# A decoder layer on one core: the cached keys and values of two head groups multiplied on GpSimd, summed on VectorE with a transposition in blocks, and TensorE adding four partial sums

## The chip, the cores and the metric

The kernel runs on 1 core of one Trainium2 chip, as one launch. The metric is the device time of that core in microseconds (us). Before the change it is 1753.67 us, the median of 3 runs (1753.51 to 1753.68).

## The reference, cut to what matters

One layer of a decoder is computed for 256 prompt tokens and for 32 sample tokens (8 sequences, "batches", of 4 new tokens each) that share all weights: one input projection (2048 to 14848 features), a gated short convolution (mixer A), attention with three head groups of 4 heads of 128 features (mixer B), two gated branch projections, an output projection, a layer norm, and a feed-forward part with 5632 inner features and a second norm. All arrays are float32.

The change concerns the sample tokens' attention to their caches. For each batch `n`, new token `t` and head `h`, a group with window 128 and dilation `dil` reads every `dil`-th earlier row:

```python
idx = l + jnp.arange(t)[:, None] - dil * j[None, :]      # j = 0 .. 128
kg = k_all[:, idx]
vg = v_all[:, idx]
sc = jnp.einsum('nthd,ntjhd->nhtj', q, kg) * ATT_SCALE - slopes * (dil * j)
...
o = jnp.einsum('nhtj,ntjhd->nthd', p / den, vg)
```

In the first group (dilation 1) the 4 new tokens of a batch share their keys and values. In groups two and three (dilations 4 and 16) each of the 4 tokens has 128 cached rows of its own, which no other token of the batch reads. So in these two groups every element of the cache that is read is multiplied with one number only: the query's feature for the keys, the softmax weight for the values. All three groups are merged by one softmax per head. The caches themselves are also outputs (moved on by four rows), so each cached element is copied once from the inputs to the outputs.

## The kernel before, in words

**Products.** Tokens lie along the free dimension (288 columns: 256 prompt, 32 sample), features on the 128 partitions. Every projection is a row of *products* (`product`, which calls `mms`): one block of 128 output features, usually 2048 inputs, so 16 blocks of 128x128. Each block takes three matmuls of 288 columns (L223 to L225), since a float32 weight is split into two float32r parts, `whi` and `wlo`, and the inputs likewise into `xh` and `xl`; so a product of 2048 inputs has 48 matmuls.

**Weights.** `prepare` loads one weight block of 1 MB by a DMA that SyncE issues (L186; tile `wst`, three buffers), and `half_block` splits it in two halves: ScalarE writes `whi` (L229) and VectorE writes `wlo` = weight minus `whi` (L229 too, inside the helper `split`). `whi` and `wlo` have four half-block buffers each. There are 297 such loads after the first three blocks. Behind some of them (`copy_rest`, L145) SyncE issues a copy of 1 MB from input to output in DRAM, 48 in all: the part of the third group's cache that is not read. That begins after load 116, behind three loads of every eleven.

**Order.** A scheduler orders each engine's instructions from the program's order and dependencies. `behind` adds an order without a wait on the engine, and `in_a_row` keeps a list of matmuls together. SyncE issues all loads, the copies and most stores from one queue, in order.

**Sample attention.** It is a generator, `sample_steps`, that `product` advances by one step per product (from the input projection's tenth or so product on), so its work is spread over about 98 products: the rest of the input projection (12 query, 24 key and value, 48 mixer A products) and a part of the first gated branch. The cache consists of 36 tiles of 128x2048 float32 (1 MB): for keys and for values 2 tiles of the first group (four batches each; called near here) and 16 of groups two and three (one batch of one group each; called far). `fetch` (L445 to L456) loads a tile into one of three buffers and later stores it from there to the output. Every eight products there is a *visit* of three tiles, 12 in all: VectorE writes, per batch, the queries (or softmax weights) with all other batches' columns set to zero (`by_batch`, L440), and TensorE multiplies these 32 columns per head with the tile (L529): 128 columns per head and batch for the near tiles, and 512 for the far ones, where all four tokens' rows are multiplied with all tokens and VectorE then picks the right quarter with a mask (`pick_t`, L461). These matmuls have float32 operands, each of which the trace records as two; the four heads use four column groups of the array, since each has 32 columns of weights. The key visits end in the softmax (L478 to L489, VectorE and ScalarE), followed by transpositions (`transposed`, L493 to L501); the value visits add up in PSUM and end in one transposition and the split into `ybh` and `ybl`, which the second gated branch reads.

**Beside it.** During the key and value products the prompt attention of each head runs in pieces between products (`prompt_attention`, L376 to L424). In mixer A each group of three products is followed by a convolution (L603 to L651): GpSimd fills the edges of `u`, ScalarE scales, and VectorE does two multiply-adds (L612), two products with PSUM operands (L635, L651) and a split.

Of the kernel before, what the change touches and what calls it, by code (L numbers as in the profile page):

```python
# [13 lines left out]
ALU = mybir.AluOpType  # L14
AX = mybir.AxisListType
# [57 lines left out]

N_WARM = 17

N_VISIT = 3
APART = 8

# [14 lines left out]
def layer_kernel(ctx: ExitStack, tc: tile.TileContext, ins, outs):  # L93
# [14 lines left out]
    def sb(pl, shape, tag, dt=F32, bufs=None):  # L108
        return pl.tile(shape, dt, tag=tag, name=nm(tag), bufs=bufs)
# [14 lines left out]
    def att(cols=512):  # L124
        return sb(ps, [P, cols], "att", bufs=2)
# [5 lines left out]
    loads = [0]  # L131
    w_load = [None]
    steps_on = [False]
    rest = [0]
    no_sync = mybir.DependencyInfo(mybir.DependencyClass.NoSync, mybir.DependencyReason.DATA)

    def behind(i, after):

        tc.add_manual_dep(i.ins, after.ins.name, no_sync, reason="pace")

    def copy_rest(after):
# [34 lines left out]
    def prepare():  # L176
        src, nk = next(w_left, (None, 0))
        if nk == 0:
            return
        st = sb(wp, [P, KD, P], "wst")  # L180
        src = src.rearrange("p (k c) -> p k c", c=P)
        loads[0] += 1

        for k0 in range(0, nk, HK if loads[0] == 1 else nk):
            k = slice(k0, k0 + (HK if loads[0] == 1 else nk))
            d = sp.dma_start(st[:, k, :], src[:, k])  # L186
        n = loads[0]
        w_load[0] = d
        if n > NB_QKV + 5 * KD and n % 11 in (0, 4, 8):
            copy_rest(d)  # L190
        w_ready.append([half_block(st, k0, min(HK, nk - k0)) for k0 in range(0, nk, HK)])

# [124 lines left out]
                            before = i  # L317
        return [t.rearrange("p a h -> p h a") for t in o]

    cst = sb(big, [P, C_BM + MASK + NT], "cst")  # L320

    pa = sb(big, [P, KD * T], "yal")

# [103 lines left out]


    bmask = cst[:, C_BM : C_BM + MASK]
    tmask = cst[:, C_BM + MASK :]  # L430

    sw_m = sb(wk, [P, 2 * NH + 1, NH, NS], "sw", bufs=1)
    dd_all = sb(big, [P, KD * T], "dd")
    kv = dd_all[:, : 2 * 2 * NG * T].rearrange("p (b c g t) -> p b c g t", b=2, c=2, g=NG)
    sw2 = dd_all[:, 2 * 2 * NG * T :]

    def by_batch(n, src, b):

        m = bmask[:, (NB - 1 - b) * NT : (NB - 1 - b) * NT + NS]
        dve.tensor_tensor(sw_m[:, n], src, m.unsqueeze(1).broadcast_to([P, NH, NS]), ALU.mult)  # L440
# [24 lines left out]
    def sample_steps():  # L465
        s = sw2[:, :SW]
# [15 lines left out]
        def softmax():  # L482
            dve.tensor_tensor(s[:, NG * P :], pn, sbias[:, NG * P :], ALU.add)
            st = sb(wk, [P, 4], "st", bufs=4)
            dve.reduce_max(st[:, 0:1], s, AX.X)
            dve.tensor_scalar_mul(st[:, 1:2], st[:, 0:1], -SCALE)
            act.activation(s, s, AF.Exp, bias=st[:, 1:2], scale=SCALE, accum_out=st[:, 2:3])
            dve.reciprocal(st[:, 3:4], st[:, 2:3])
            dve.tensor_scalar_mul(s, s, st[:, 3:4])  # L489
# [10 lines left out]
            in_a_row(row)  # L500
            act.copy(vn, pv[: NG * NS].rearrange("p (j d) -> p j d", j=NH))  # L501

        for values in range(2):
            p = [None] * NG
            for first in range(0, N_CT, N_VISIT):
                here = held[first : first + N_VISIT]
                for n in range(APART):
                    fetch()
                    if values and first == 0 and n == 3:
                        transposed()  # L510
                    if n == APART - 2:
                        at = 0
# [6 lines left out]
                for g, batches in here:  # L519
                    c = cache_tiles.pop(0)  # L520
                    cols = P if g == 0 else NT * P
                    for b in batches:
                        if b == 0:

                            p[g] = p[1] if values and g == 2 else att(P) if g == 0 else (
                                att() if g == 2 else sb(ps, [P, cols], "long", bufs=1))
                        o = (b % 4) * NH * P if g == 0 else 0
                        for j in range(NH):
                            row.append(pe.matmul(  # L529
                                p[g][j * NS : (j + 1) * NS], sw_m[:, len(row) // NH, j], c[:, o + j * cols : o + (j + 1) * cols],  # L530
                                start=b == 0 and not (values and g == 2), stop=b == NB - 1 and not (values and g < 2),
                            ))
                rest_of = [g for g, batches in here if NB - 1 in batches]
                if values and 0 in rest_of:

                    row += [
                        pe.matmul(
                            p[0][j * NS : (j + 1) * NS], sTn[:, j * NS : (j + 1) * NS], vn[:, j, :], start=False, stop=True
                        )
                        for j in range(NH)  # L540
                    ]
                elif not values and NG - 1 in rest_of:

                    pn = att(NG * NS)
                    row += [
                        pe.matmul(
                            pn[j * NS : (j + 1) * NS, k * NS : (k + 1) * NS], q_s[:, k, j, :], k_s[:, k, j, :],
                            start=True, stop=True,
                        )
                        for k in range(NG) for j in range(NH)  # L550
                    ]
# [10 lines left out]
        yield  # L562
        po = att(P)
        pe.transpose(po, o_sb, ident)
        oT = sw_m[:, 0].rearrange("p j r -> p (j r)")
        act.copy(oT, po)
        split(*(h3(t)[:, :, :, P:] for t in (ybh, ybl)), oT.rearrange("p (j a h) -> p j h a", j=NH, h=2))
        yield

    steps = sample_steps()  # L570

# [2 lines left out]
    for j in range(NH):  # L574
        for g in range(NG):
            act.copy(h2(q_all[:, j, g]), q_first.pop(0) if q_first else product(x))
            if j == 1 and g == 1:
                load_distances()
            elif j == 1:
                for dst, src in ((prm, ins["prm"]),) if g else (  # L580
                    (cst[:, :C_BM], ins["cst"][:, :C_BM]),
                    (cst[:, C_BM : C_BM + MASK], ins["cst"][:, C_MASK : C_MASK + MASK]),
                    (cst[:, C_BM + MASK :], ins["cst"][:, C_TM:C_M0]),
                ):
                    behind(sp.dma_start(dst, src), w_load[0])
            steps_on[0] = j * NG + g >= NH * NG - 2 - APART // 2
        pool.tensor_copy(q_s[:, :, j, :].rearrange("p g (a h) -> p g h a", h=2), h3(q_all[:, j])[:, :, :, P:])
    for j in range(NH):
        kT, vT = (kv[:, j % 2, c] for c in range(2))
# [479 lines left out]
```

## Time and profile before

| | |
|---|---|
| median of 3 runs | 1753.67 us (1753.51 to 1753.68) |
| the profiled execution's own time | 1753.35 us |
| its span in the trace | 1751.6 us |
| mean granted TensorE clock | 0.996 |
| ScalarE busy | 799.4 us (46%), 1149 instructions |
| moved by DMA | 436.15 MB, mean 249 GB/s |
| HBM read / written | 389.79 MB / 94.53 MB |

Times in the trace are counted from the span's start. PE is TensorE's matmuls, PEld its weight loads (beside the matmuls), DVE is VectorE, ACT ScalarE, POOL GpSimd, SP SyncE ("SPq" its queue of DMA issues). A group's row gives line, engine, operation, output and inputs, shapes, count, then busy time in us and mean ns of one, then how long the engine was idle just before and what ended that. A timeline's row gives start and duration in us. In a table by stretches, each engine has its busy time within the stretch; the last three columns are the granted clock, the busy share of the 16 DMA engines and what they moved. The matmuls are pipelined, so the 286 ns of one overlap with the next.

### The profile page before, as it was taken

To read this page: it belongs to the slowest core of one execution; us is meant where nothing else is said; L and a number is where in the kernel's file an instruction comes from. 1 tells how busy PE (TensorE), PEld (TensorE's weight loads), DVE (VectorE), ACT (ScalarE), POOL (GpSimd) and SP (SyncE) were. 2 spreads that over 40 slices of the span, in tenths; PEclk is the share of its full clock that TensorE was granted. 3 is DMA by queue.
4 is the path that set the end of the run, shared out by engine and by line. 5 is a ranking of instruction groups with operands and counts; after the bars stand their busy time and mean duration, and the time that the engine had idled before them with its cause. 6 is when DMAs were issued, how large, how long until landed. Compare 5 with 4: busy or idle time off the path is not lost.

```text
span 1751.6 us, 33565 instructions
## 1 busy us (share of the span) xinstructions
PE 1735.7 (99%) x14256; PEld 1710.6 (98%) x14256; DVE 1012.4 (58%) x1329; ACT 799.4 (46%) x1149; POOL 242.9 (14%) x404
## 2 busy tenths in 40 slices
PE   9999999999999999999999999999999999999996
PEld 9999999999999999999999999999999999999996
DVE  5444445565555444455688888865555555555554
ACT  6444443343334333344455655544454443345444
POOL 0000000000000000001165323300011110011155
PEclk9999999999999999999999999999999999999998
DMA  9887777877777784467756666566666666666662
GB/s 352 299 324 284 250 274 291 310 303 281 280 282 284 306 313 169 157 247 276 283 218 234 223 223 234 217 234 223 229 229 224 234 220 238 218 236 220 220 219 106
DMA packets 63046, 436.15 MB, mean 249 GB/s; under 512 B 7728, under 2 KB 11312, under 8 KB 19120
## 3 DMA queue, kind: packets, MB, share of 16 engines
q1 hardware_dynamic: 61456, 429.89, 66.8%
q10 hardware_dynamic: 1440, 4.13, 0.6%
q8 instruction: 111, 1.82, 0.4%
q14 instruction: 39, 0.32, 0.1%
HBM read 389.79 MB, written 94.53 MB: 277 GB/s over the span
## 4 chain that ended last, share of the span: by engine, by line
PE 99%; DVE 0%; DMA 0%; ACT 0%; issue 0%; DVEq 0%
PE acc L223 32%; PE acc L224 31%; PE acc L225 31%; PE long L529 1%; PE acc L311 1%; PE att L529 1%; PE att L418 0%; DMA dd<-in_w_in 0%; DVE dd L763 0%; PE att L378 0%; PE acc L410 0%; PE att L376 0%; ACT yah L773 0%; PE att L401 0%; DVE yah L772 0%; PE att L727 0%
## 5 line engine op out<-in xcount | busy, mean ns | idle before, releaser
L229 DVE TENSOR_TENSOR wlo<-wst,whi 128x1024 fp32r<-128x1024 f32 (+1 forms) x578 | 706.5, 1223 | 595.9 <-ACT whi L229 592.5
L229 ACT CAST whi<-wst 128x1024 fp32r<-128x1024 f32 (+1 forms) x578 | 590.6, 1022 | 879.9 <-PE acc L224 775.8
L223 PE MATMUL acc<-xh,whi 128*128 128x288 f32 (+1 forms) x3216 | 923.2, 287 | 0.0
L224 PE MATMUL acc<-xl,whi 128*128 128x288 f32 (+1 forms) x3216 | 921.1, 286 | 0.0
L225 PE MATMUL acc<-xh,wlo 128*128 128x288 f32 (+1 forms) x3216 | 921.1, 286 | 0.0
L223 PEld LDWEIGHTS acc<-xh,whi 128*128 128x128 f32 x3216 | 608.5, 189 | 6.1 <-issue 6.1
L224 PEld LDWEIGHTS acc<-xl,whi 128*128 128x128 f32 x3216 | 608.5, 189 | 0.0
L225 PEld LDWEIGHTS acc<-xh,wlo 128*128 128x128 f32 x3216 | 608.5, 189 | 0.0
L223 PE MATMUL acc<-yah,whi 128*128 128x288 f32 x1216 | 348.2, 287 | 0.0
L224 PE MATMUL acc<-yal,whi 128*128 128x288 f32 x1216 | 348.1, 286 | 0.0
L225 PE MATMUL acc<-yah,wlo 128*128 128x288 f32 x1216 | 348.1, 286 | 0.0
L223 PEld LDWEIGHTS acc<-yah,whi 128*128 128x128 f32 x1216 | 230.0, 189 | 2.5 <-issue 2.5
L225 PEld LDWEIGHTS acc<-yah,wlo 128*128 128x128 f32 x1216 | 230.1, 189 | 0.0
L224 PEld LDWEIGHTS acc<-yal,whi 128*128 128x128 f32 x1216 | 230.0, 189 | 0.0
L624 POOL COPY qk_s<-u 128x2 f32<-128x2 f32 x44 | 37.8, 860 | 571.6 <-ACT u L846 448.8
L612 DVE SCALAR_TENSOR_TENSOR cy<-u,prm,cy 128x304 f32<-128x304 f32 x120 | 73.7, 614 | 3.8 <-ACT cy L610 0.7
L683 POOL TENSOR_TENSOR ya<-ya,dd 128x288 f32<-128x288 f32 x16 | 13.7, 855 | 304.6 <-DVE ya L682 299.0
L635 DVE TENSOR_TENSOR ya<-cy,acc 128x256 f32<-128x256 f32 x88 | 23.5, 311 | 34.1 <-PE acc L225 34.1
L229 ACT CAST yah<-ya 128x288 fp32r<-128x288 f32 x76 | 32.6, 429 | 17.6 <-POOL ya L683 9.2
L624 POOL COPY cm<-u 128x2 f32<-128x2 f32 x16 | 2.9, 184 | 252.7 <-DVE u L651 252.7
L717 POOL TENSOR_TENSOR cache<-cache,dd 128x288 f32<-128x288 f32 x29 | 29.0, 1001 | 52.6 <-DVE dd L811 33.5
L229 DVE TENSOR_TENSOR yal<-ya,yah 128x288 fp32r<-128x288 f32 x76 | 35.1, 461 | 1.2 <-ACT yah L229 1.2
(181 smaller groups left out, 832.5 us busy)
## 6 DMA issues: line engine op xcount, KB each, us to landing
wst<-in_w_in SPq DMA_DIRECT2D x112, 1024.0 KB, 5.5
wst<-in_w_up SPq DMA_DIRECT2D x88, 1024.0 KB, 4.8
wst<-in_w_down SPq DMA_DIRECT2D x32, 1024.0 KB, 4.8
cache<-in_ck SPq DMA_DIRECT2D x18, 1024.0 KB, 8.3
out_o_ck<-cache SPq DMA_DIRECT2D x18, 1024.0 KB, 7.5
cache<-in_cv SPq DMA_DIRECT2D x18, 1024.0 KB, 7.1
out_o_cv<-cache SPq DMA_DIRECT2D x18, 1024.0 KB, 8.9
wst<-in_w_a SPq DMA_DIRECT2D x16, 1024.0 KB, 5.6
```

Of the source, the lines that this page charges most:

```text
L223: pe.matmul(out, hi[:, c, :], xh_k, start=k == 0, stop=False)
L224: pe.matmul(out, hi[:, c, :], xl_k, start=False, stop=False)
L225: last_mm[0] = pe.matmul(out, lo[:, c, :], xh_k, start=False, stop=k == nk - 1)
L229: return act.copy(hi, src), dve.tensor_tensor(lo, src, f32(hi), ALU.subtract)
L311: i = pe.matmul(o[b], first_w(term == 2, b, k), xk, start=k == 0 and term == 0, stop=k == KD - 1 and term == 2,)
L529: row.append(pe.matmul(p[g][j * NS : (j + 1) * NS], sw_m[:, len(row) // NH, j], c[:, o + j * cols : o + (j + 1) * cols], start=b == 0 and ...
L612: dve.scalar_tensor_tensor(y, u[:, i : i + YW], prm[:, w0 + i : w0 + i + 1], y, ALU.mult, ALU.add)
L624: pool.tensor_copy(dst[:, 0:2], u[:, SEQ : SEQ + 2])
L635: dve.tensor_tensor(a, b, c, ALU.mult)
L683: pool.tensor_tensor(m, m, ma[:, i], ALU.add)
L717: pool.tensor_tensor(self.s1, self.s1, d, ALU.add)
```

## The change

The far tiles are no longer multiplied by TensorE. GpSimd multiplies a loaded tile in place, in two instructions of 128x1024, with the query's features (or the softmax weights) of the tile's batch, one number per head and token broadcast over 128 columns (`weighted`). VectorE then sums each half over 32 partitions at a time, by a reduction with a transposition of 32x32 blocks (`folded`, two instructions of 128x1024 per tile). What is left per head, token and batch are four partial sums (one per block of 32 partitions, `NQ`), and TensorE adds them by small float32 matmuls with a constant `sel` of 128x32, four identities on top of each other: 32 for the scores (in `scores`) and 8 for the output (in `output`). The near tiles keep their matmuls, 32 for the keys in one row with the small ones (`scores`), and 32 for the values (`near_output`). The masks of `by_batch` are written for the near tiles alone, and `pick_t` and its mask are gone.

Tiles are loaded two per five products (`PACE`), the far keys first, then the near tiles, then the far values; a tile is multiplied three products after its load is issued and summed in the next two (`LATER`). Since the tile is changed in place, the caches are no longer stored from the buffers: their 36 copies go from DRAM to DRAM with the 48 others, behind three weight loads of every ten from load 20 to load 297. In the changed kernel's order TensorE has the 128-column near matmuls in two rows, 32 and 8 small matmuls, and nothing else of the sample attention moves on TensorE. The diff, cut to its core:

```diff
-N_VISIT = 3
-APART = 8
+NQ = P // 32
+PACE = 5, 2
+LATER = 3
...
     def copy_rest(after):
-        if rest[0] < N_REST:
-            n = rest[0]
-            rest[0] += 1
-            behind(sp.dma_start(outs["o_rest"][n], ins["rest"][n]), after)
+        if copies:
+            behind(sp.dma_start(*copies.pop()), after)
...
-        if n > NB_QKV + 5 * KD and n % 11 in (0, 4, 8):
+        if n >= 20 and n % 10 in (0, 3, 7):
             copy_rest(d)
...
-    def by_batch(n, src, b):
-        m = bmask[:, (NB - 1 - b) * NT : (NB - 1 - b) * NT + NS]
-        dve.tensor_tensor(sw_m[:, n], src, m.unsqueeze(1).broadcast_to([P, NH, NS]), ALU.mult)
-    cache_left = iter([(which, n) for which in ("ck", "cv") for n in range(N_CT)])
-    cache_tiles = []
-    to_store = []
-    def fetch():
-        if to_store:
-            sp.dma_start(*to_store.pop())
-        elif len(cache_tiles) < N_VISIT:
-            which, n = next(cache_left, (None, 0))
-            if which:
-                t = sb(wk, [P, 2048], "cache", bufs=3)
-                behind(sp.dma_start(t, ins[which][n]), w_load[0])
-                to_store.append((outs["o_" + which][n], t))
-                cache_tiles.append(t)
-    def pick_t(out, p, add):
-        for t in range(NT):
-            dve.scalar_tensor_tensor(
-                out, p[:, t * P : (t + 1) * P], tmask[:, t : t + 1], add if t == 0 else out, ALU.mult, ALU.add
+    def by_batch(src):
+        for b in range(NB):
+            m = bmask[:, (NB - 1 - b) * NT : (NB - 1 - b) * NT + NS]
+            dve.tensor_tensor(sw_m[:, b], src, m.unsqueeze(1).broadcast_to([P, NH, NS]), ALU.mult)
+    def half_tile(tile, h):
+        n = NH // 2 * NT * P
+        return tile[:, h * n : (h + 1) * n]
+    def weighted(tile, w):
+        n = NH // 2
+        for h in range(2):
+            t = half_tile(tile, h).rearrange("p (j t c) -> p j t c", j=n, t=NT)
+            i = pool.tensor_tensor(
+                t, t, w[:, h * n : (h + 1) * n].unsqueeze(3).broadcast_to([P, n, NT, P]), ALU.mult
             )
+            behind(i, w_split[1])
+    def folded(out, tile, h):
+        n = NH // 2
+        behind(dve.tensor_reduce(
+            out[:, h * n : (h + 1) * n].rearrange("p j q t -> p j t q"),
+            half_tile(tile, h).rearrange("p (j t q c) -> p j t q c", j=n, t=NT, c=32),
+            AX.X, ALU.add, apply_transpose=True,
+        ), w_split[1])
...
-        held = [(0, range(4)), (0, range(4, NB))] + [(g, (b,)) for g in range(1, NG) for b in range(NB)]
-        def scored(g, p):
-            sg = s[:, g * P : (g + 1) * P]
-            if g == 0:
-                dve.tensor_tensor(sg, p, sbias[:, :P], ALU.add)
-            else:
-                pick_t(sg, p, sbias[:, g * P : (g + 1) * P])
-        def softmax():
-            dve.tensor_tensor(s[:, NG * P :], pn, sbias[:, NG * P :], ALU.add)
+        sums_k, sums_v = (
+            t[:, : (NG - 1) * NB * NH * NT * NQ].rearrange("p (g j q r) -> p g j q r", g=NG - 1, j=NH, q=NQ)
+            for t in (sw2, sw_m.rearrange("p n j r -> p (n j r)"))
+        )
...
+        far = [(1 + n // NB, n % NB) for n in range((NG - 1) * NB)]
+        tiles = [("ck", 2 + n) for n in range(len(far))] + [("ck", 0), ("ck", 1), ("cv", 0), ("cv", 1)]
+        tiles += [("cv", 2 + n) for n in range(len(far))]
...
+        def near(p, last):
+            row = []
+            for half in range(2):
+                c = here.pop(min(here))
+                for b in range(half * NB // 2, (half + 1) * NB // 2):
+                    for j in range(NH):
+                        o = (b % (NB // 2) * NH + j) * P
+                        row.append(pe.matmul(
+                            p[j * NS : (j + 1) * NS, :P], sw_m[:, b, j], c[:, o : o + P],
+                            start=b == 0, stop=last and b == NB - 1,
+                        ))
+            return row
+        def scores():
+            p = att(SW)
+            row = near(p, True)
+            row += [
+                pe.matmul(
+                    p[j * NS : (j + 1) * NS, (1 + g) * P + q * 32 : (1 + g) * P + (q + 1) * 32], sums_k[:, g, j, q],
+                    sel, start=True, stop=True,
+                )
+                for g in range(NG - 1) for q in range(NQ) for j in range(NH)
+            ]
+            row += [
+                pe.matmul(
+                    p[j * NS : (j + 1) * NS, NG * P + k * NS : NG * P + (k + 1) * NS], q_s[:, k, j, :], k_s[:, k, j, :],
+                    start=True, stop=True,
+                )
+                for k in range(NG) for j in range(NH)
+            ]
+            in_a_row(row)
+            dve.tensor_tensor(s, p, sbias, ALU.add)
...
-        for values in range(2):
-            p = [None] * NG
-            for first in range(0, N_CT, N_VISIT):
-                here = held[first : first + N_VISIT]
-                for n in range(APART):
...
-                            for b in batches:
-                                by_batch(at, sT[:, g].rearrange("p (j r) -> p j r", j=NH) if values else q_s[:, g], b)
-                                at += 1
...
-                row = []
-                for g, batches in here:
-                    c = cache_tiles.pop(0)
-                    cols = P if g == 0 else NT * P
-                    for b in batches:
-                        if b == 0:
-                            p[g] = p[1] if values and g == 2 else att(P) if g == 0 else (
-                                att() if g == 2 else sb(ps, [P, cols], "long", bufs=1))
-                        o = (b % 4) * NH * P if g == 0 else 0
-                        for j in range(NH):
-                            row.append(pe.matmul(
-                                p[g][j * NS : (j + 1) * NS], sw_m[:, len(row) // NH, j], c[:, o + j * cols : o + (j + 1) * cols],
-                                start=b == 0 and not (values and g == 2), stop=b == NB - 1 and not (values and g < 2),
-                            ))
-                rest_of = [g for g, batches in here if NB - 1 in batches]
-                if values and 0 in rest_of:
...
-                in_a_row(row)
-                for g in rest_of:
-                    if not values:
-                        scored(g, p[g])
-                    elif g == 0:
-                        act.copy(o_sb, p[0])
-                    elif g == NG - 1:
-                        pick_t(o_sb, p[g], o_sb)
-            if not values:
-                softmax()
-        yield
...
+        def near_output():
+            p = att(P)
+            row = near(p, False)
+            row += [
+                pe.matmul(p[j * NS : (j + 1) * NS], sTn[:, j * NS : (j + 1) * NS], vn[:, j, :], start=False, stop=True)
+                for j in range(NH)
+            ]
+            in_a_row(row)
+            act.copy(o_sb, p)
+        def output():
+            po = att(2 * P)
+            far_o = by_row(po[:, P:])
+            row = [pe.transpose(po[:, :P], o_sb, ident)]
+            row += [
+                pe.matmul(
+                    far_o[q * 32 : (q + 1) * 32], sel, sums_v[:, g, :, q],
+                    start=g == 0, stop=g == NG - 2,
+                )
+                for g in range(NG - 1) for q in range(NQ)
+            ]
+            in_a_row(row)
+            oT = sw_m[:, NB].rearrange("p j r -> p (j r)")
+            act.copy(oT, po[:, :P])
+            dve.tensor_tensor(oT, oT, po[:, P:], ALU.add)
+            split(*(h3(t)[:, :, :, P:] for t in (ybh, ybl)), oT.rearrange("p (j a h) -> p j h a", j=NH, h=2))
...
+        load = [n * PACE[0] // PACE[1] for n in range(len(tiles))]
+        n_k = len(far) + 2
...
+        for n in range(len(tiles)):
+            if n < len(far) or n >= n_k + 2:
+                for d, what in enumerate(("weighted", 0, 1)):
+                    todo.setdefault(load[n] + LATER + d, []).append((what, n))
+        at = load[n_k - 1] + LATER
+        for n, what in (
+            (at - 2, "masked q"), (at, scores), (at + 2, transposed), (at + 3, "masked p"), (at + 5, near_output),
+            (load[-1] + 2 * LATER, output),
+        ):
+            todo.setdefault(n, []).append((what, None))
+        for n in range(load[-1] + 2 * LATER + 1):
...
+                    which, k = tiles[i]
+                    here[i] = sb(wk, [P, 2048], "cache", bufs=3)
+                    behind(sp.dma_start(here[i], ins[which][k]), w_load[0])
+            for what, i in todo.get(n, ()):
+                if i is not None:
+                    g, b = far[i if i < n_k else i - n_k - 2]
+                    rows = slice(b * NT, (b + 1) * NT)
+                    if what == "weighted":
+                        weighted(here[i], (q_s[:, g] if i < n_k else by_row(sT[:, g]))[:, :, rows])
+                    else:
+                        folded((sums_k if i < n_k else sums_v)[:, g - 1, :, :, rows], here[i], what)
+                        if what == 1:
+                            here.pop(i)
...
-            steps_on[0] = j * NG + g >= NH * NG - 2 - APART // 2
+            steps_on[0] = j * NG + g >= NH * NG - 1 - LATER
```

More of the change, by code (lines that the diff above doesn't have):

```diff
@@ L139, in behind @@
         tc.add_manual_dep(i.ins, after.ins.name, no_sync, reason="pace")
+    copies = [(outs["o_rest"][n], ins["rest"][n]) for n in range(N_REST)]
+    copies += [(outs["o_" + c][n], ins[c][n]) for n in range(N_CT) for c in ("ck", "cv")]
     def copy_rest(after):
-        if rest[0] < N_REST:
-            n = rest[0]
-            rest[0] += 1
-            behind(sp.dma_start(outs["o_rest"][n], ins["rest"][n]), after)
+        if copies:
+            behind(sp.dma_start(*copies.pop()), after)
     w_split = []
@@ L318, in first_three @@
         return [t.rearrange("p a h -> p h a") for t in o]
-    cst = sb(big, [P, C_BM + MASK + NT], "cst")
+    cst = sb(big, [P, C_BM + MASK], "cst")
+    sel = sb(big, [P, 32], "sel")
     pa = sb(big, [P, KD * T], "yal")
@@ L429, in layer_kernel @@
     bmask = cst[:, C_BM : C_BM + MASK]
-    tmask = cst[:, C_BM + MASK :]
-    sw_m = sb(wk, [P, 2 * NH + 1, NH, NS], "sw", bufs=1)
+    sw_m = sb(wk, [P, NB + 1, NH, NS], "sw", bufs=1)
     dd_all = sb(big, [P, KD * T], "dd")
@@ L501, in transposed @@
             act.copy(vn, pv[: NG * NS].rearrange("p (j d) -> p j d", j=NH))
-        for values in range(2):
-            p = [None] * NG
-            for first in range(0, N_CT, N_VISIT):
-                here = held[first : first + N_VISIT]
-                for n in range(APART):
[L508 to L512, printed above, removed]
-                        for g, batches in here:
-                            for b in batches:
-                                by_batch(at, sT[:, g].rearrange("p (j r) -> p j r", j=NH) if values else q_s[:, g], b)
-                                at += 1
-                    yield
-                row = []
-                for g, batches in here:
-                    c = cache_tiles.pop(0)
-                    cols = P if g == 0 else NT * P
-                    for b in batches:
-                        if b == 0:
-                            p[g] = p[1] if values and g == 2 else att(P) if g == 0 else (
-                                att() if g == 2 else sb(ps, [P, cols], "long", bufs=1))
-                        o = (b % 4) * NH * P if g == 0 else 0
-                        for j in range(NH):
-                            row.append(pe.matmul(
-                                p[g][j * NS : (j + 1) * NS], sw_m[:, len(row) // NH, j], c[:, o + j * cols : o + (j + 1) * cols],
-                                start=b == 0 and not (values and g == 2), stop=b == NB - 1 and not (values and g < 2),
-                            ))
-                rest_of = [g for g, batches in here if NB - 1 in batches]
-                if values and 0 in rest_of:
[L536 to L551, printed above, removed]
-                in_a_row(row)
-                for g in rest_of:
-                    if not values:
-                        scored(g, p[g])
-                    elif g == 0:
-                        act.copy(o_sb, p[0])
-                    elif g == NG - 1:
-                        pick_t(o_sb, p[g], o_sb)
-            if not values:
-                softmax()
@@ L562, in sample_steps, with by_row @@
[L562 to L568, printed above, removed]
+        def by_row(t):
+            return t.rearrange("p (j r) -> p j r", j=NH)
+        def near_output():
[7 more added lines that the diff above has]
+            act.copy(o_sb, p)
@@ new lines, in sample_steps @@
+        for i, o in enumerate(range(0, P, 32)):
+            if i == 1:
+                dve.tensor_tensor(sel, ident[:, :32], ident[:, 32:64], ALU.add)
+            elif i:
+                dve.tensor_tensor(sel, sel, ident[:, o : o + 32], ALU.add)
+        load = [n * PACE[0] // PACE[1] for n in range(len(tiles))]
+        n_k = len(far) + 2
+        todo = {}
+        for n in range(len(tiles)):
+            if n < len(far) or n >= n_k + 2:
+                for d, what in enumerate(("weighted", 0, 1)):
+                    todo.setdefault(load[n] + LATER + d, []).append((what, n))
@@ new lines, in sample_steps @@
+        at = load[n_k - 1] + LATER
[5 more added lines that the diff above has]
+        for n in range(load[-1] + 2 * LATER + 1):
+            for i in range(len(tiles)):
+                if load[i] == n:
+                    which, k = tiles[i]
[11 more added lines that the diff above has]
+                            here.pop(i)
+                elif what == "masked q":
+                    by_batch(q_s[:, 0])
+                elif what == "masked p":
+                    by_batch(by_row(sT[:, 0]))
+                else:
+                    what()
+            yield
```

3 lines of the change are left out of this document (1 added, 2 removed).

## The prediction

> **What bounds the kernel now.** I read the page first: the engines' shares and the chain that ended last.
>
> ```profile
> span 1751.6 us, 33565 instructions
> ...
> PE 1735.7 (99%) x14256; PEld 1710.6 (98%) x14256; DVE 1012.4 (58%) x1329; ACT 799.4 (46%) x1149; POOL 242.9 (14%) x404
> ...
> PE 99%; DVE 0%; DMA 0%; ACT 0%; issue 0%; DVEq 0%
> ```
>
> TensorE is the bound and nothing else comes near. Shares are averages, though, so I looked at stretches: two of the sample attention, the one with the most crowded DMA, one behind it, and the one where VectorE and GpSimd are fullest.
>
> ```profile
> 100.00:114.00 14.00, 14.00 (x117) 14.00 (x116) 5.73 (x5) 5.83 (x7) 1.02 (x1) 1.00 1.01 391
> ...
> 420.00:670.00 250.00, 250.00 (x2044) 239.10 (x2044) 122.94 (x154) 95.72 (x112) 3.89 (x28) 1.00 0.77 293
> 670.00:860.00 190.00, 190.00 (x1553) 190.00 (x1553) 99.29 (x111) 81.96 (x110) 13.67 (x16) 1.00 0.63 221
> 860.00:960.00 100.00, 100.00 (x818) 100.00 (x817) 82.44 (x87) 50.69 (x74) 53.53 (x47) 1.00 0.66 242
> ...
> 520.00:555.24 35.24, 35.24 (x290) 35.24 (x289) 18.32 (x26) 14.44 (x18) 1.11 (x8) 1.00 0.90 347
> ```
>
> In each the first column behind the length, TensorE's, equals the length: no gap, at full clock, not even with VectorE at 82% and GpSimd at 54% (860 to 960), nor with the DMA engines full (100 to 114). So whatever leaves TensorE's list shortens the kernel at once, as long as its weights still come in time. From 670 to 860 a matmul takes 190.00 / 1553 = 0.1223 us, a product of 48 takes 5.87 us.
>
> **What is removed from TensorE.** The chain of waits gives the visits and their parts:
>
> ```profile
> 94.54 1.88 PE att L529 x64
> 96.42 0.86 PE long L529 x8
> ...
> 367.54 0.19 PE att L546 x24
> ...
> 418.58 0.22 PE att L537 x8
> ...
> 515.99 2.71 PE long L529 x24
> 518.70 0.32 PE acc L223
> ...
> 565.94 2.71 PE long L529 x24
> ```
>
> Two visits of three far tiles start 565.94 - 515.99 = 49.95 us apart, with eight products between: 49.95 - 8 x 48 x 0.1223 = 2.97 us per visit. Of this 2.71 are the matmuls (0.90 per far tile) and 0.26 the change of kind at both ends (0.20 of it behind: the next product's first matmul counts 0.32 instead of 0.12). The near tiles with one far tile take 1.88 + 0.86 = 2.74, about the same. Twelve visits: 12 x 2.97 = 35.6 us.
>
> What stays or comes: two rows of near matmuls, 2 x (1.88 + 0.26) = 4.3 us. The 32 small matmuls of the scores are 64 records of the very shape of L546 (32 columns of weights, 32 moving, four column groups): 64 x 0.19 / 24 = 0.5. The 8 of the output are 16 records of 128 columns like L537's: 16 x 0.22 / 8 = 0.4. The rows L546, L537 and the transpositions are in both kernels. Sum 35.6 - 5.2 = **30.4 us less** on TensorE. Bounds of the small ones: nothing from below; from above, each of the 80 records at the 0.1223 us of a 288-column matmul on the whole array, 9.8 us. L546 (0.008 us a record) is this very shape, so I take it.
>
> **What is added, and what covers it.** GpSimd gets 64 multiplications of 128x1024, VectorE 64 reductions of 128x1024. Nearest rows:
>
> ```profile
> L229 DVE TENSOR_TENSOR wlo<-wst,whi 128x1024 fp32r<-128x1024 f32 x12 | 14.7, 1226 | 15.3 <-ACT whi L229 15.3
> ...
> L825 DVE SCALAR_TENSOR_TENSOR h<-cache,wgb,h 128x288 f32<-128x288 f32 x32 | 17.1, 535 | 1.1
> L440 DVE TENSOR_TENSOR sw<-qk_s,cst 128x128 f32<-128x128 f32 x24 | 6.1, 291 | 4.2 <-PE long L529 2.4 <-PE att L529 1.5 <-POOL qk_s L587 0.2
> L392 DVE TENSOR_REDUCE st<-yal 128x1 f32<-128x512 f32 x8 | 5.1, 680 | 0.0
> ...
> 1737.48 8.34 POOL L763 TENSOR_TENSOR dd<-dd,cache 128x576 f32<-128x576 f32 x6 [4.42 <-ACT cache L758]
> ```
>
> GpSimd: 8.34 / 6 = 1.39 us for 576 columns, also with a broadcast operand, so 2.47 us for 1024. VectorE: a plain reduction of 512 takes 0.68 and a 1024-column instruction 1.23, so 1.3 us without the transposition (at most 2 x 0.68 = 1.36). The trace has no reduction with a transposition; if blocks are turned in a pass of their own it is 2.7. I take 1.3, since a row of this operation on this engine is nearest. [...]
>
> The rate: two tiles in five products is 1.2 tiles in three, a mixer A period of 17.6 us. VectorE has 18.32 / 2 = 9.2 us of work per period now (row 520 to 555). Added: 2.4 x 1.3 = 3.1, sum 12.3, or 70%. GpSimd: 2.4 x 2.47 = 5.9 us, 34%. Less on VectorE: 32 masks of 0.29 (L440) and 16 picks, some 14 us over all. None of this is on TensorE's path by itself.
>
> The two engines are not independent, however:
>
> ```profile
> 899.70 1.78 POOL L803 TENSOR_TENSOR h<-xh,xl 128x288 f32<-128x288 f32 x1
> 901.45 1.01 POOL L718 TENSOR_TENSOR cache<-cache,cy 128x288 f32<-128x288 f32 x1
> ...
> 899.36 1.47 DVE L229 TENSOR_TENSOR wlo<-wst,whi 128x1024 fp32r<-128x1024 f32 x1 [0.56 <-ACT whi L229]
> 900.75 1.05 DVE L813 SCALAR_TENSOR_TENSOR xl<-dd,prm,xh 128x288 fp32r<-128x288 f32 x1
> 901.72 1.05 DVE L810 SCALAR_TENSOR_TENSOR h<-h,cache 128x288 f32<-128x288 f32 x1
> ```
>
> L813 and L810 take 1.05 where the same shape takes 0.535 alone (L825), and L803 1.78 where 288 / 576 x 1.39 = 0.70 is its due: L803 stands until `wlo` ends at 900.83, L813 until L803 ends at 901.48, and so on. Instructions with two SBUF inputs take turns. A `wlo` that meets a multiplication thus waits up to 2.47 us, and per period at most 5.9. VectorE would have 12.3 + 5.9 = 18.2 at the very worst, over the 17.6, and 12.3 if every wait falls into idle time; I take half, 15.2 (86%), about the 82% of 860 to 960, where TensorE has no gap.
>
> **How late may a `wlo` be?**
>
> ```profile
> 504.15 1.05 ACT L229 CAST whi<-wst 128x1024 fp32r<-128x1024 f32 x1 [1.85 <-PE acc L224]
> ...
> 505.23 1.23 DVE L229 TENSOR_TENSOR wlo<-wst,whi 128x1024 fp32r<-128x1024 f32 x1 [0.35 <-ACT whi L229]
> ```
>
> ScalarE starts at 504.15, when TensorE has ended the half block of four before; three halves of 2.94 us follow, so this one is wanted at 504.15 + 8.8 = 512.97, and it is ready at 506.46: 6.5 us to spare. Two multiplications (4.9 us) and a sum (1.3) come to 6.2 if all fall on one `wlo`, just inside, and they take turns with the splits. Only where a prompt head's softmax falls in too (four times) I expect a gap of some tenths; I put 1 us in for them.
>
> **Queues.** SyncE loses 36 stores that wait for their own load and gets 36 copies that wait for no data; its loads into tile buffers now wait for the second sum, which lies two products ahead (11.7 us). On GpSimd the convolution's small fills stand behind multiplications, with a whole period to spare, as two `u` buffers are filled ahead. The payload per product is 1 MB of weights, 0.4 of tiles and 0.3 of copies, 1.7 x 1.05 MB / 5.87 us = 304 GB/s; by 0.77 at 293 and 0.63 at 221 (this one with copies) the DMA engines are 80 to 87% busy, less than in bursts that now pass without a gap. The last copy goes behind the last weight load:
>
> ```profile
> 1689.11 26.17 SPq L186 DMA_DIRECT2D wst<-in_w_down  x7
> 1741.45 6.29 SPq L796 DMA_DIRECT2D out_o_y<-yah  x7
> ...
> out_o_rest<-in_rest SPq DMA_DIRECT2D x48, 7.0
> ```
>
> It is issued near 1715 (1689.11 + 26.17), lands 7 us later, and the outputs start at 1741: hidden.
>
> **Sum.** The profiled execution took 1753.35 us, 0.3 below the median. 1753.35 - 30.4 + 1 = **1724 us**.
>
> **Rivals.**
> - *Taking turns holds up TensorE.* If all 5.9 us of a period fall on VectorE, it needs 18.2 where TensorE needs 17.6: 3.4% of the 79 products (464 us) of multiplying, 16 us: 1753.4 - 30.4 + 16 = 1739. For it: the rows at 900. Against it: sums and PSUM operands (L651, L635) can run beside GpSimd. [...]
> - *Slower: the sum is dear.* At 2.7 us a sum, VectorE needs 9.2 + 6.5 + 4.4 (three quarters of the turns) = 20.1 of 17.6 us, and the 464 us grow by 66: 1753.4 - 30.4 + 66 = 1789. It decides against the change from 17.6 x (1 + 30.4 / 464) = 18.8 us per period on, with these turns a sum of 2.2 us.
> - *Weights late.* If each of some 26 copies during the multiplying held TensorE for 1 us, 1753.4 - 30.4 + 26 = 1749. Against it: 100 to 114.
> - *It doesn't do what it says*: the 80 small records take a whole matmul's time each, and TensorE keeps more of the work than counted: 1753.4 - 35.6 + 4.3 + 9.8 = 1732.
>
> **How the numbers follow.** Forecast 0.66, with its own range 1720 to 1731; turns 0.15; dear sum 0.12; late weights 0.04; small matmuls 0.03. What a measurement can tell from no change is 0.2%, 3.5 us. Faster: 0.66 + 0.15 + 0.03 + half of the late weights = 0.86; same the other half, 0.02; slower 0.12. The forecast, the turns and the small matmuls hold 0.84, so the range goes from 1718 (all changes of kind cost more than counted) to 1746.
>
> **What would show it.** Right: TensorE without a gap from 100 to 640, no L529-like row of 512 columns, sums at 1.2 to 1.4 us, multiplications near 2.5, and `wlo` above 1.23 on the mean in this stretch. Wrong: sums above 2 us, TensorE's idle time put down to `wlo`, or ScalarE waiting for `wst` loads.

## The result, and the profile after

The changed kernel takes 1726.78 us (median of 4 runs, 1726.2 to 1726.9) where the kernel before takes 1753.64 beside it: a ratio of 0.9846, with a 95% interval of 0.9829 to 0.9863, 26.9 us less. The forecast was 1724 within 1718 to 1746. The profiled execution of the changed kernel took 1726.74 us, its span is 1725.0.

From the page of the changed kernel, its span, its engines and its memory traffic:

```profile
span 1725.0 us, 33346 instructions
...
PE 1706.4 (99%) x14080; PEld 1703.5 (99%) x14080; DVE 1127.8 (65%) x1352; ACT 799.4 (46%) x1149; POOL 405.3 (23%) x468
...
HBM read 427.53 MB, written 94.53 MB: 303 GB/s over the span
```

TensorE is still the bound, with 29.3 us less of busy time (1735.7 - 1706.4). VectorE has 115 us more, GpSimd 162 us more. Where TensorE stands still now, by the table of waits of that engine, and the stretches of the sample attention:

```profile
PE acc L228 <- DVE wlo L232: 1.8, 1, 1.8
PE acc L244 <- DVE cy L241: 1.2, 1, 1.2
PE att L515 <- issue: 0.5, 1, 0.5
PE acc L314 <- ACT whi L281: 0.4, 1, 0.4
PE acc L314 <- ACT xh L287: 0.4, 1, 0.4
```

```profile
20.00:94.00 74.00, 72.22 (x590) 72.01 (x589) 43.47 (x40) 32.20 (x43) 17.73 (x13) 1.00 0.71 252
94.00:268.00 174.00, 174.00 (x1423) 173.57 (x1423) 122.55 (x143) 78.52 (x119) 48.61 (x30) 1.00 0.77 293
268.00:420.00 152.00, 151.52 (x1420) 150.88 (x1420) 109.77 (x132) 62.97 (x81) 37.74 (x46) 1.00 0.75 284
420.00:640.00 220.00, 220.00 (x1808) 219.63 (x1807) 166.34 (x163) 89.77 (x106) 76.51 (x54) 1.00 0.80 298
```

The wait for `cy` at the start, 1.2 us, is as before. Two waits of 0.4 us in the first row of products (L314) are the first weights' and inputs' splits. New in the sample attention are one gap of 1.8 us, put down to a weight split, and 0.5 us in the row of the scores. From 94 us on TensorE has no other gap in these stretches, with VectorE at 70 to 76%.

The new instructions, in the groups by shape:

```profile
L456 POOL TENSOR_TENSOR cache<-cache,dd 128x1024 f32<-128x1024 f32 x32 | 77.1, 2429 | 40.4 <-DMA cache<-in_cv 39.3 <-DVE wlo L232 1.1
L456 POOL TENSOR_TENSOR cache<-cache,qk_s 128x1024 f32<-128x1024 f32 x32 | 73.6, 2321 | 7.8 <-DMA cache<-in_ck 7.7
L465 DVE TRANSPOSE_TENSOR_REDUCE dd<-cache 128x32 f32<-128x1024 f32 x32 | 39.6, 1237 | 0.0
L465 DVE TRANSPOSE_TENSOR_REDUCE sw<-cache 128x32 f32<-128x1024 f32 x32 | 39.6, 1237 | 0.0
...
L232 DVE TENSOR_TENSOR wlo<-wst,whi 128x1024 fp32r<-128x1024 f32 x546 | 716.6, 1314 | 451.1 <-ACT whi L232 449.2
```

A sum with its transposition takes 1.237 us, as long as a plain instruction of 1024 columns (1.226 for a split in the kernel before). A multiplication takes 2.3 to 2.4 us on the mean, turns included. A split of 1024 columns takes 1.314 us on the mean over the whole kernel.

The gap, in the timelines of VectorE, GpSimd and TensorE of the changed kernel:

```profile
78.11 1.22 DVE L232 TENSOR_TENSOR wlo<-wst,whi 128x1024 fp32r<-128x1024 f32 x1 [1.72 <-ACT whi L232]
79.50 10.21 DVE L445 TENSOR_TENSOR sw<-qk_s,cst 128x128 f32<-128x128 f32 x8 [0.16 <-POOL qk_s L632]
89.63 2.35 DVE L232 TENSOR_TENSOR wlo<-wst,whi 128x1024 fp32r<-128x1024 f32 x2
```

```profile
79.55 9.61 POOL L456 TENSOR_TENSOR cache<-cache,qk_s 128x1024 f32<-128x1024 f32 x5
```

```profile
88.84 0.29 PE L227 MATMUL acc<-xl,whi 128*128 128x288 f32 x1
90.90 0.39 PE L228 MATMUL acc<-xh,wlo 128*128 128x288 f32 x1 [1.78 <-DVE wlo L232]
```

The eight key masks (`by_batch`, L445) stand near 80 us, not by the scores near 345: the program asks for them late, but they depend on the queries alone, and the scheduler put them there. Five multiplications start at the same moment. A mask of 0.29 us has two SBUF inputs and takes turns with 1.9 us of GpSimd: five of the eight last 1.98 us each, one beside each multiplication, and three last 0.28 to 0.29. Together they take 10.21 us instead of 2.3. The split behind them comes too late, and TensorE waits 90.90 - 88.84 - 0.12 = 1.94 us.

### The profile page after: what moved, and what is told of

The parts are those of the page before. It is cut to its first block, busy times and chain, and to the rows that moved or that the text cites. A ratio compares the mean times of both kernels' runs of the same rounds, so it can differ in the third digit from the quotient of the medians.

```text
span 1725.0 us, 33346 instructions
## 1 busy us (share of the span) xinstructions
PE 1706.4 (99%) x14080; PEld 1703.5 (99%) x14080; DVE 1127.8 (65%) x1352; ACT 799.4 (46%) x1149; POOL 405.3 (23%) x468
## 4 chain that ended last, share of the span: by engine, by line
PE 98%; DVE 1%; DMA 0%; ACT 0%; issue 0%; SPq 0%; DVEq 0%
PE acc L226 32%; PE acc L228 32%; PE acc L227 32%; PE acc L314 1%; PE att L423 0%; DMA wst<-in_w_in 0%; DVE dd L808 0%; PE att L497 0%; PE att L383 0%; PE acc L415 0%; PE att L381 0%; DVE sw L445 0%; ACT yah L818 0%; PE att L406 0%; DVE wlo L232 0%
## 5 line engine op out<-in xcount | busy, mean ns | idle before, releaser
L232 DVE TENSOR_TENSOR wlo<-wst,whi 128x1024 fp32r<-128x1024 f32 (+1 forms) x578 | 739.7, 1281 | 472.9 <-ACT whi L232 470.9
L456 POOL TENSOR_TENSOR cache<-cache,dd 128x1024 f32<-128x1024 f32 x32 | 77.1, 2429 | 40.4 <-DMA cache<-in_cv 39.3
L657 DVE SCALAR_TENSOR_TENSOR cy<-u,prm,cy 128x304 f32<-128x304 f32 x120 | 77.5, 646 | 4.2 <-ACT cy L655 1.1
L456 POOL TENSOR_TENSOR cache<-cache,qk_s 128x1024 f32<-128x1024 f32 x32 | 73.6, 2321 | 7.8 <-DMA cache<-in_ck 7.7
L232 DVE TENSOR_TENSOR yal<-ya,yah 128x288 fp32r<-128x288 f32 x76 | 41.9, 552 | 1.3 <-ACT yah L232 1.1
L680 DVE TENSOR_TENSOR ya<-cy,acc 128x256 f32<-128x256 f32 x88 | 23.4, 306 | 28.1 <-PE acc L228 28.1
```

The source lines that it names most:

```text
L232: return act.copy(hi, src), dve.tensor_tensor(lo, src, f32(hi), ALU.subtract)
L456: i = pool.tensor_tensor(t, t, w[:, h * n : (h + 1) * n].unsqueeze(3).broadcast_to([P, n, NT, P]), ALU.mult)
L657: dve.scalar_tensor_tensor(y, u[:, i : i + YW], prm[:, w0 + i : w0 + i + 1], y, ALU.mult, ALU.add)
L680: dve.tensor_tensor(a, b, c, ALU.mult)
```

## The experiments

The theory: the gain comes from TensorE's shorter list alone; the work given to GpSimd and VectorE is hidden, but for the gap at the masks. Rivals: the relieved queue of SyncE pays a part; turns with GpSimd cost small amounts all over; the new work stands near a bound, so that a somewhat dearer sum would cost much. All ratios are to the kernel before, beside which each was run, with their 95% intervals. All experiments but `e1_copies` hold the edit of `e2_masks`.

**The copies alone (`e1_copies`).** In the kernel before:

```diff
-            sp.dma_start(*to_store.pop())
+            to_store.pop()
...
-        if n > NB_QKV + 5 * KD and n % 11 in (0, 4, 8):
+        if n >= 20 and n % 10 in (0, 3, 7):
             copy_rest(d)
```

and `copy_rest` takes the 84 copies of the change.

> The kernel before, with the stores of the cached tiles from the buffers replaced by the change's copies from DRAM to DRAM at its places (84 copies, behind three loads of every ten); TensorE, GpSimd and VectorE as before. Theory (the time comes from TensorE's shorter list alone): 1753.6 us, within 1 us. Rival (the queue relieved of 36 waiting stores gives a good part of the 26.9 us): 1740 us or less. If the 80 to 87% busy DMA engines hurt: above 1757 us.

Measured: 1753.48 us beside 1753.51, ratio 1.0 (0.9991 to 1.0009). The DMA part of the change is worth nothing and costs nothing; the rival of the relieved queue is out.

**The masks in their place (`e2_masks`).** In the changed kernel:

```diff
-            dve.tensor_tensor(sw_m[:, b], src, m.unsqueeze(1).broadcast_to([P, NH, NS]), ALU.mult)
+            i = dve.tensor_tensor(sw_m[:, b], src, m.unsqueeze(1).broadcast_to([P, NH, NS]), ALU.mult)
+            behind(i, w_split[1])
```

> The changed kernel, with the masks of the near tiles kept in the order behind the split of the weights of their own step, so that the eight key masks no longer stand near 80 us beside the first multiplications. Theory (the 2.06 us gap of TensorE at 88.84 us comes from these masks taking turns with GpSimd): the gap goes, 1724.7 us (2.1 less). Rival (the multiplications alone delay the splits there): the gap stays or moves, 1726 to 1727 us.

Measured: 1724.2 us (1724.11 to 1724.36), ratio 0.9833 (0.9818 to 0.9848), the fastest kernel of the study. The masks' groups and TensorE's waits in it:

```profile
L445 DVE TENSOR_TENSOR sw<-dd,cst 128x128 f32<-128x128 f32 x8 | 1.8, 285 | 0.0
L445 DVE TENSOR_TENSOR sw<-qk_s,cst 128x128 f32<-128x128 f32 x8 | 1.7, 285 | 0.0
```

```profile
PE acc L244 <- DVE cy L241: 1.2, 1, 1.2
PE att L516 <- issue: 0.5, 1, 0.5
```

The masks take 1.7 us again, and no gap is put down to a split. The multiplications are still there, so they alone did not make the gap. Of the 2.6 us, 1.94 are the gap. Some 0.5 more lie ahead of it: the first row of matmuls (L314) ends at 24.20 us in the changed kernel and at 23.68 here. That is not the masks' doing: the row ends at 24.29 in the profile of `e7_fold3` and at 24.24 in that of `e8_nowork`, both with the masks in their place. What sets it is open.

**No multiplications (`e3_nomult`).** The call of `weighted` becomes `pass`.

> As e2_masks, and the multiplications on GpSimd are left out, so that the sums are of unweighted caches. Theory (taking turns with GpSimd costs TensorE nothing once the masks are away): the same as e2_masks within 0.7 us, with the mean of the weight splits of 1024 columns back from 1.31 to 1.25 us. Rival (turns cost time in many small gaps): 1 to 3 us below e2_masks.

Measured: 1724.8 us, ratio 0.9836 (0.9821 to 0.9851), within 0.6 of `e2_masks`, as the theory had it; the mean of a split of 1024 columns is 1.248 us. The page's lines of the engines, first of `e2_masks`, then of `e3_nomult`:

```profile
PE 1706.4 (99%) x14080; PEld 1703.8 (99%) x14080; DVE 1118.9 (65%) x1352; ACT 799.3 (46%) x1149; POOL 405.8 (24%) x468
```

```profile
PE 1706.5 (99%) x14080; PEld 1704.2 (99%) x14080; DVE 1073.7 (62%) x1352; ACT 799.4 (46%) x1149; POOL 251.0 (15%) x404
```

GpSimd loses 155 us. VectorE has the same 1352 instructions and takes 45 us less for them, so these 45 us were waiting for turns. TensorE's busy time does not move, and neither does the time. Turns are real, and hidden.

**Neither multiplications nor sums (`e8_nowork`).** `weighted` is left out as above, and `folded` gives way to one fill per set of sums:

```diff
-                        folded((sums_k if i < n_k else sums_v)[:, g - 1, :, :, rows], here[i], what)
+                        if what == 0 and i in (0, n_k + 2):
+                            behind(dve.memset((sw2 if i < n_k else ...)[:, :1024], 0.5), w_split[1])
```

> As e2_masks, with neither multiplications nor sums: both are left out, and two fills of constant values stand for all sums. The tiles are still loaded and TensorE's list is the same. Theory (TensorE's list sets the time and the 79 us of sums on VectorE and 154 us on GpSimd are hidden wholly): 1724.2 us within 0.7. Rival (they cost a little all over): 1 to 4 us less.

Measured: 1724.83 us, ratio 0.9837 (0.9823 to 0.9852). All the computing that the change adds outside TensorE, taken away, brings nothing, and the copies are worth nothing either (`e1_copies`). What is left of the change, TensorE's list, is the whole gain.

**The multiplications on VectorE (`e5_multdve`).** In `weighted`, `pool.tensor_tensor` becomes `dve.tensor_tensor`.

> As e2_masks, with the multiplications on VectorE in place of GpSimd. Theory: VectorE has 9.2 + 2.4 x 1.23 + 2.4 x 1.24 = 15.1 of 17.6 us per three products, no turns are taken, TensorE stays fed: the same as e2_masks within 1 us (about 1725). Rival (GpSimd is what makes the change possible, since VectorE can't hold both): TensorE gaps put down to the weight splits, 1735 us or more.

Measured: 1724.61 us, ratio 0.9836 (0.9819 to 0.9852). The stretch of the values, and the group:

```profile
420.00:636.00 216.00, 216.00 (x1775) 215.63 (x1774) 172.62 (x187) 87.91 (x104) 7.86 (x26) 1.00 0.77 297
```

```profile
L457 DVE TENSOR_TENSOR cache<-cache,qk_s 128x1024 f32<-128x1024 f32 x32 | 37.5, 1212 | 0.0
```

VectorE is 80% busy with all of it (172.62 of 216), and TensorE has no gap. So GpSimd is not needed here: it saves VectorE 75 us of multiplying and costs it 45 us of waiting.

**Every sum twice (`e4_fold2`).** `for _ in range(2):` ahead of `folded`.

> As e2_masks, with every sum with a transposition on VectorE issued twice, so that a sum costs 2.5 us. This is the rival of the dear sum made real. The prediction's reckoning (three quarters of the turns on VectorE): 9.2 + 2.4 x 2.47 + 4.4 = 19.5 of 17.6 us per three products, 464 us grow by 11%, about 1775 us. Reckoning by the turns measured in the changed kernel (VectorE's splits, multiply-adds and masks wait some 45 us against 151 us of GpSimd's multiplying, a third): 9.2 + 5.9 + 1.8 = 16.9 of 17.6, TensorE fed but for a few gaps: 1725 to 1732 us.

Measured: 1729.94 us, ratio 0.9868 (0.9851 to 0.9884), 5.7 us over `e2_masks`, as reckoned by the measured turns and far from the 1775 of the prediction's reckoning. TensorE's waits:

```profile
PE acc L415 <- DVE yal L401: 3.5, 3, 1.6
PE att L516 <- issue: 1.6, 1, 1.6
```

3.5 us are at the prompt heads' softmax (`yal`, L401), where the forecast had expected gaps at single sums. The other 1.6 are a stop in the row of the scores for which the trace names no cause; it was 0.5 in `e2_masks`.

**Every sum three times (`e7_fold3`).** `range(3)`.

> As e2_masks, with every sum issued three times (3.7 us per sum). Theory (TensorE pays as soon as VectorE's work per three products passes 17.6 us): VectorE was 202.19 of 216 us busy, 94% or 16.5 us a period, from 420 to 636 with two sums; a third adds 2.4 x 1.24 = 3.0, so 19.5 of 17.6, and the 464 us of multiplying grow by 8 to 10%: 37 to 48 us more than e4_fold2's 1730, about 1767 to 1778 us, slower than before. Rival (VectorE has slack that its busy time hides, since its waits for turns shrink): below 1750 us.

Measured: 1747.84 us (1746.62 to 1751.48), ratio 0.9972 (0.9961 to 0.9983). Two stretches, and TensorE's longest waits:

```profile
94.00:268.00 174.00, 164.17 (x1299) 162.65 (x1299) 152.91 (x171) 72.69 (x110) 40.73 (x28) 0.97 0.72 264
...
420.00:655.00 235.00, 228.81 (x1845) 226.34 (x1844) 234.38 (x232) 90.51 (x109) 83.14 (x61) 1.00 0.76 283
```

```profile
PE acc L415 <- DVE yal L401: 9.8, 5, 3.6
PE acc L228 <- DVE wlo L232: 6.4, 12, 1.2
```

From 420 to 655 VectorE is the bound: it is busy 234.38 of 235 us. The larger part of the waits, 9.8 us, is at the prompt heads' softmax, though, in a stretch where VectorE has idle time left and where the granted clock was 0.97 (174 x 0.03 = 5 us more, an estimate). In all the kernel is 23.6 us over `e2_masks`, where 43 to 54 were expected, and the number is the rival's (below 1750). The rival's reason shows too: over the whole kernel the 546 splits of 1024 columns take 723.8 us in `e4_fold2` (1.329 each) and 718.2 in `e7_fold3` (1.317). So the splits wait less for turns once VectorE is full, 5.6 us less in all, where the expectation had added the third sum to the same waits. From 2.5 to 3.7 us per sum the time grows by 17.9 us; at that slope, an estimate, the gain would be gone at about 4.1 us per sum.

**Every multiplication twice (`e6_mult2`).** `for _ in range(2):` ahead of `weighted`.

> As e2_masks, with every multiplication on GpSimd issued twice (the tile is weighted twice, so the sums are others). GpSimd then holds 4.8 x 2.4 = 11.5 us per three products, VectorE's instructions with two SBUF inputs 8.6 us: 20.1 of 17.6 us if they exclude each other wholly. Theory (exclusive turns): GpSimd falls behind, VectorE's in-order sums wait for it, the splits come late, TensorE gets gaps: some 40 to 70 us more, 1765 to 1795 us. Rival (the turns only overlap in part, or the waits fit into VectorE's idle time): below 1735 us.

Measured: 1729.83 us, ratio 0.9867 (0.9852 to 0.9881), 5.6 us over `e2_masks`: far from the theory's 1765 to 1795, and within the rival's number (below 1735). The stretch of the values, and one tile in the timelines of GpSimd and VectorE:

```profile
420.00:636.00 216.00, 212.94 (x1731) 212.08 (x1730) 208.74 (x162) 85.83 (x103) 161.27 (x85) 1.00 0.78 298
```

```profile
443.65 9.63 POOL L457 TENSOR_TENSOR cache<-cache,dd 128x1024 f32<-128x1024 f32 x4
```

```profile
443.99 2.63 DVE L232 TENSOR_TENSOR wlo<-wst,whi 128x1024 fp32r<-128x1024 f32 x1
446.55 1.23 DVE L466 TRANSPOSE_TENSOR_REDUCE sw<-cache 128x32 f32<-128x1024 f32 x1
447.71 0.98 DVE L232 TENSOR_TENSOR yal<-ya,yah 128x288 fp32r<-128x288 f32 x1
448.62 5.75 DVE L232 TENSOR_TENSOR wlo<-wst,whi 128x1024 fp32r<-128x1024 f32 x2
```

VectorE is at 97%, and the splits wait as exclusive turns would have it: 5.75 us for two that take 2.46 alone. But the price was wrong. The shortest multiplication takes 1.89 us, here and in the changed kernel (minimum, median and maximum of the 32 on values in the changed kernel: 1890, 2734, 2978 ns); the 2.4 us of the expectation were a mean that held turns already. By an estimate with 1.89, 4.8 x 1.89 + 8.6 = 17.7 of 17.6 us, the two just fit. And the sum at 446.55 beside a multiplication takes 1.23 us as ever: it takes no turns. TensorE's waits for splits come to 3.1 us here, in three gaps, and the stop in the row of the scores to 1.3.

## Why the prediction was right

The measured time lies 2.8 us above the forecast. 0.9 of that are in the gap. The other 1.9 lie in TensorE's list and at the start of the kernel, for which the sum has no term: the first row of matmuls ends at 23.98 us in the profile of the kernel before, and in others at 23.68 (`e2_masks`) to 24.29 (`e7_fold3`).

**TensorE's list, 30.4 us less.** Right. Without the gap at the masks the change brings 1753.51 - 1724.20 = 29.3 us. Most of the 1.1 us between lies in the small matmuls. The chain of waits of `e2_masks`:

```profile
344.07 1.88 PE att L498 x64
345.96 0.57 PE att L508 x46
346.59 0.47 issue
347.06 0.39 PE att L516 x22
347.45 0.32 PE acc L226
...
633.18 0.57 PE att L562 x16
633.75 0.32 PE acc L226
```

The row of the scores lasts 347.45 + 0.32 - 344.07 = 3.70 us; by the forecast's terms it would be 1.88 + 0.51 + 0.19 + 0.32 = 2.90. So 0.8 more, of which 0.47 is a stop ahead of its last 22 records for which the trace names no cause (0.2 to 1.6 us in the kernels here). The output's 16 records take 0.57 instead of 0.44; the rest is within what two runs differ by (1752.96 to 1753.71 for the kernel before, beside `e2_masks`). 46 of the small records take 0.57 us, 0.012 us each, so the rival in which each takes a whole matmul's 0.1223 us did not happen.

**The price of a sum, 1.3 us.** Right: 1.237, and the rival's 2.7 did not happen. 1024 columns cost about the same with the transposition as a split without it (1.226). A sum takes no part in the turns either: it takes 1.23 to 1.24 us beside GpSimd's multiplications (`e6_mult2`) and without them (`e5_multdve`). The same holds for a product of 256 columns with a PSUM operand (L680 in the changed kernel): 0.41 to 0.44 us in the 10 places where a multiplication runs beside it, and as much in the other 34.

**The price of a multiplication, 2.47 us.** Too high: 1.89 for the shortest. That the mean with turns, 2.3 to 2.4, came near the 2.47 is chance. The row it came from (L763) is of another shape and of another broadcast, along the middle instead of the innermost dimension; which of the two makes the difference was not tried.

**Turns cost VectorE half of GpSimd's time, 3 us per period.** Right in kind, too high in size: 45 us over 79 products are 1.7 us per three. VectorE came to 70 to 76% instead of 86%, and that is why `e4_fold2` stayed far below the prediction's reckoning of the dear sum, and why the point from which that rival decides, put at 2.2 us per sum, lies near 4 by the estimate above. So TensorE was spared in spite of two wrong sizes, by room that VectorE had in either case. The rival in which the turns hold up TensorE came true in one place, the gap at the masks: one of the prediction's own signs of being wrong, idle time put down to `wlo`, is there for 1.8 us.

**1 us of gaps, at the prompt heads.** Wrong in size and place. The gap was 1.94 us, and it stood at the masks. The prediction had entered masks only as work that VectorE loses, and 32 of the 48 did go; where the 16 that stay would stand, it did not ask. The scheduler put the eight key masks 265 us ahead of their use, to the place where the multiplications begin. The changed kernel's order on VectorE, without any run, would have shown this. At the prompt heads there was no gap until the sums were doubled.

**The slack of a split, 6.5 us.** The gap bears it out. ScalarE's part of the split that came late, in the changed kernel:

```profile
79.97 1.05 ACT L232 CAST whi<-wst 128x1024 fp32r<-128x1024 f32 x1 [1.60 <-PE acc L227]
```

VectorE's part could have begun at 81.02 and began at 89.63, 8.6 us late; less the slack of 6.5 that makes 2.1 us, and TensorE waited 1.94.

**Queues and DMA, 80 to 87% busy.** Right that they are hidden: 71 to 80% in the stretches above, a little less than reckoned, and `e1_copies` shows no difference. From 42 to 640 us the changed kernel's table of waits has none of ScalarE for a `wst` load, so the rival of late weights did not happen.

## What to carry to other kernels

Where one engine has no gap, a change's gain is what leaves that engine's list; here this could be summed from the chain of waits to about 1 us in 30. The rest is to find the few places where the hidden work delays that engine's inputs: look at where the scheduler puts the small instructions that have few dependencies, and count each small instruction with two SBUF inputs that meets a large one of GpSimd at GpSimd's duration, not at its own (1.98 us here, not 0.29). A price taken from another row should be taken from its shortest instance, since a mean can hold waits (2.4 us here, 1.89 for the shortest).

## What was not expected of the hardware

- GpSimd multiplies 1024 columns in 1.89 us at the shortest (1.85 ns a column) where the operand is broadcast along the innermost dimension, against 8.34 / 6 / 576 = 2.41 ns a column in the row before.
- Eight instructions of 0.29 us on VectorE lasted 10.21 us beside five multiplications of GpSimd: the two engines alternated, one instruction each, and five of the eight took 1.98 us.
- A reduction of 1024 columns with a transposition of 32x32 blocks takes 1.237 us on VectorE, as long as a plain instruction of 1024 columns (1.23).
- In `e7_fold3` the granted TensorE clock fell to 0.97 on the mean from 94 to 268 us, a stretch in which TensorE stood still for 10 of 174 us; from 420 to 655, with 6 of 235 us, it stayed at 1.00.
